# The end of attention in another order, two low parts moved from POOL to DVE, and a sum of two products kept in PSUM

## The chip, the cores and the metric

The kernel runs on one core of one Trainium2 chip. The time is the device time of one execution in microseconds (us), over everything from the first to the last instruction; the figure for a kernel is the median of several runs. The core's engines are named as in the profile: PE (matmuls), DVE (the vector engine), ACT (the scalar engine, with its function tables), POOL (GpSimd) and SP, which issues the loads. Each engine works through its own list in the order written; engines wait for one another through semaphores. SBUF is the memory on the chip, PSUM the banks that PE writes into.

## The reference

One layer of a decoder trunk on 512 tokens of width 1024, in float32. Three sub-layers, each with a norm before it and a norm after it, and a residual sum:

```python
x = x + 0.5 * rms_norm(swiglu(rms_norm(x, ffn1_pre_g), ffn1_w_gu, ffn1_w_down), ffn1_post_g)
y = hybrid_mixer(rms_norm(x, mix_pre_g), w_in, ..., w_o)
x = x + rms_norm(y, mix_post_g)
x = x + 0.5 * rms_norm(swiglu(rms_norm(x, ffn2_pre_g), ffn2_w_gu, ffn2_w_down), ffn2_post_g)
```

`swiglu` is `(silu(x @ w_gate) * (x @ w_up)) @ w_down` with an inner width of 2816. The mixer projects to five parts with `w_in`: `x_lru` and `gate_lru` (512 columns each), queries (8 heads of 64), keys and values (2 heads of 64). The LRU half is a short convolution, two block-diagonal gates, a linear scan over the tokens, times `gelu(gate_lru)`. The attention half is a causal window of 128 tokens with sinks. Each half has its own norm, and both together are multiplied by `w_o`.

## The kernel before

**Products.** The activations lie transposed, `xT[c]` being 128 features by 512 tokens for c = 0 to 7. Float32 accuracy comes from splitting every operand in a high part (rounded to the matmul's format, by an ACT copy) and a low part (what is left, by a subtraction), and from three matmuls (`mm3`, L358 to L363): high by high, high by low, low by high. Weights pass through class `Weights`: a unit is loaded by SP, rounded by ACT (`round`, L171) and split by the `low` engine (`take_low`, L176). `W.fill(n)` makes the low parts of all units up to n beyond those taken, and calls the loads that follow; where it is called decides where in the list of DVE or POOL the low part stands. Which of the two does it is written beside each unit: for `w_in`'s columns 2 and 3 (`xl`) DVE and POOL, and for the first pair of ffn2's gate and up weights DVE for gate 0 and POOL for up 0, gate 1 and up 1.

**Feed-forward products by quads.** Most of the pairs of hidden chunks go through `quad` (L682), a product by seven 2x2 block products with sums of blocks of weights and of tokens. It uses three banks, A, D and B. `seven` takes a weight unit and runs 24 matmuls into one bank. Block product b11 goes into A and is copied by ACT to `p1` (L691); later b21 goes into B, and a DVE addition (L697) forms `p1 + B`, on which ACT runs the Silu one unit later. There are nine quads in ffn1 (names ending in a) and eight in ffn2 (b).

**Boundaries.** `boundary` (L560) joins a sub-layer's last products to the next sub-layer's first ones. Of the eight output chunks, the last three (5, 6, 7, called late) are made in two halves of 256 tokens. While the three products of half 1 run, half 0 gets its norm: `stats` (four small matmuls on the sum of squares `accb_r`, L406, then a square root on ACT and a reciprocal and a diagonal `dg_r` on DVE), `spread` (L421, a matmul that gives the inverse norm to all partitions), `scale` (L554, DVE), `add` (L558, the residual sum, DVE for even chunks and POOL for odd ones) and `high` (L431, ACT, the high part of the next input, `xh_mx` or `xh_f`). Calls are put between the row steps of a product by `hooks`: a product has `n` steps of three matmuls, n = 6 at the first boundary (ffn1 to mixer) and 8 at the second (mixer to ffn2). Then `k_high` (L374) runs the next sub-layer's first four products row by row: for each row k it multiplies the high part of that row by high and low parts of the four weight units, eight matmuls a row; the low parts of the rows follow in `k_low`. In row steps 0 to 3, `k_high` starts as soon as `xh` of row 0 is there, and takes rows 1 to 3 as they come.

**The end of attention.** Eight units of scores, softmax and values run in a software pipeline (L1292 on), with the last weight products of the gate (`gt`) between them on PE. Beside them the LRU half goes on: the scans (L1172, four of them, `scan(2)`, `scan(3)`, then `scan(0)` and `scan(1)`), and gelu of the gate in four steps which end in `G` (L1128) for chunks 0 and 1. `run_due` issues what has been put off to a given unit; `deferred` holds one subtraction, the low part `wlo_wo` of the fourth chunk of `w_o` (L157), to be issued by `deferred.run()`. After the last unit, `invert_rms` scales the four blocks `yn` by their norm (L1287), PE transposes them (`atp`, L1338), ACT and DVE make high and low parts (`yah`, `yal`), POOL multiplies the scans by G or gt (L1364), and DVE sums the squares in `acc_lru` (L1358), for which PE's statistics `rms_lru` (L406) wait. PE works on the attention rows of `w_o` in between (L1380, L1383).

Of the kernel before, what the change touches and what calls it, by code (L numbers as in the profile page):

```python
# [11 lines left out]
AF = mybir.ActivationFunctionType  # L12
# [7 lines left out]
KD = D // P  # L20
F = 2816
# [90 lines left out]
def tile_layer(ctx: ExitStack, tc: tile.TileContext, out: bass.AP, **ins: bass.AP):  # L112
# [73 lines left out]
        return add_pair([src[0, r0 * P:(r0 + nk) * P, c * P:(c + 2) * P]], nk, f"{name}{c}_", low)  # L186

    def add_gate_up(w_gu, f, name):
        g, u = (add_cols(w_gu[:, :, o:o + F], f, KD, f"{name}{s}", 0, (dve, dve) if f else (dve if s == "g" else pool, pool))
                for s, o in (("g", 0), ("u", F)))  # L190
        for j in range(2):
            g[j]()
            u[j]()
# [47 lines left out]
    O2 = 2 * C  # L241
    O3 = O2 + C
    for c in (0, 2):
        for add in add_cols(w_in, c, KD, "xl", 0, (dve, pool)):
            add()
    for add in add_pair([w_in[0, :, O3:O3 + 2 * P]], KD, "kv"):
        add()
# [123 lines left out]
            mm3(ps[:, sl], w, k, [t[:, sl] for t in x], k == 0, k == len(xs) - 1)  # L371
        return ps

    def k_high(ws, banks, xs, sl, ks):  # L374


        for k in ks:
            xh = xs[k][0][:, sl]
            for (hi, lo), ps in zip(ws, banks):
                pe.matmul(ps[:, sl], hi[:, k, :], xh, start=k == 0, stop=False)  # L380
                pe.matmul(ps[:, sl], lo[:, k, :], xh, start=False, stop=False)  # L381

    def k_low(ws, banks, xs, sl):
        n = len(xs)
# [119 lines left out]
    class Residual:  # L504
# [48 lines left out]
            y = self.ys[c][:, HALF[h]]  # L553
            dve.scalar_tensor_tensor(y, y, self.gain(c), bc, op0=ALU.mult, op1=ALU.mult)  # L554

        def add(self, c, h):
            sl = HALF[h]
            (pool if c % 2 else dve).tensor_add(xT[c][:, sl], self.ys[c][:, sl], xT[c][:, sl])  # L558

    def boundary(res, late, xs, parts, nxt, name):  # L560

        for i, (c, w) in enumerate(late):
            b = product(w, xs, HALF[0], f"{name}y{c}0")
            res.late(c, b, parts and parts[c], 0)
            res.late_square(c, 0)
            res.late_add(0, i == 0)
            W.fill((2, 3, 3)[i])

        def steps(ks, h, bc):
            for k in ks:  # L570
                res.scale(k, h, bc)
            for k in ks:
                res.add(k, h)
            for k in ks:
                nxt.high(k, h)

        bcs = [None, None]

        def spread(h):
            bcs[h] = res.rms[h].spread()  # L580

        def spread_a():
            spread(0)
            steps((0, 1), 0, bcs[0])

        n = len(xs)
        hooks = [{}, {1: res.rms[0].stats, 3: lambda: W.fill(4), n - 2: spread_a}, {}]
        for i, (c, w) in enumerate(late):
            b = product(w, xs, HALF[1], f"{name}y{c}1", hooks[i])
            if i == LATE - 1:  # L590
                for k in (2, 3):
                    res.scale(k, 0, bcs[0])
                res.add(2, 0)
                res.add(3, 0)
                res.late_add(1, False)
            res.late(c, b, parts and parts[c], 1)
            if i == LATE - 1:
                nxt.high(2, 0)
            res.late_square(c, 1)
            if i == 0:  # L600
                res.late_add(1, True)
        res.scale(4, 0, bcs[0])
        res.late_add(1, False)
        nxt.high(3, 0)
        res.scale(5, 0, bcs[0])
        for k in (4, 5):
            res.add(k, 0)
        for k in (4, 5):
            nxt.high(k, 0)
        ws = [W.take(0) for _ in range(4)]  # L610
        banks = [bank(f"{name}n{i}") for i in range(4)]
        k_high(ws, banks, nxt.xs, HALF[0], range(0, 4))
        for k in (6, 7):
            res.scale(k, 0, bcs[0])
        for k in (6, 7):
            res.add(k, 0)
        res.rms[1].stats()
        for k in (6, 7):
            nxt.high(k, 0)
        for k in range(KD):  # L620
            nxt.low(k, 0)
        k_high(ws, banks, nxt.xs, HALF[0], range(4, 6))
        spread(1)
        for k in range(0, KD, 2):
            steps((k, k + 1), 1, bcs[1])
        nxt.sum_squares(0)
        k_high(ws, banks, nxt.xs, HALF[0], range(6, 8))
        k_low(ws, banks, nxt.xs, HALF[0])
        for k in range(KD):
            nxt.low(k, 1)  # L630
        W.fill(2)
        nxt.sum_squares(1)
        k_high(ws, banks, nxt.xs, HALF[1], range(8))
        k_low(ws, banks, nxt.xs, HALF[1])
        return banks


    class Hidden:
# [24 lines left out]
        def quad(self, f, last, ahead):  # L663
# [24 lines left out]
            A, D, B = (bank(f"{s}{n}") for s in "adb")  # L688
            p1, p7, u2, u4, g1 = (wt(f"{s}{n}") for s in ("p1", "p7", "u2", "u4", "g1"))
            seven(A, "b11", True)  # L690
            act.copy(p1, A)  # L691
            seven(D, "t3", True)
            act.copy(p7, D)
            seven(A, "t2", False)
            act.copy(u2, A)
            seven(B, "b21", True)
            dve.tensor_add(p1, p1, B)  # L697
            W.later(1, act.activation, p1, p1, AF.Silu)
            seven(A, "t1", False)
            act.copy(u4, A)  # L700
            W.later(1, dve.tensor_add, u4, p7, u4)
# [592 lines left out]
    for now in range(n_units + 2):  # L1294
# [19 lines left out]
        if now == 6:  # L1314
            for ci in range(KC):
                root_u(ci)
            for ci in (2, 3):
                scan(ci)
        if now == n_units:
            scan(0)  # L1320
            deferred.run()
            preload(AF.Sqrt)
            root_rms(slice(0, NB - 1))

# [2 lines left out]
    preload(AF.Exp)  # L1327
    invert_rms(slice(0, NB - 1))
    invert_rms(slice(NB - 1, NB))
    scan(1)  # L1330
    run_due(n_units + 1)
    pump(100)
    ysp = [None] * KD
    gts[KC - 1] = scaled(wt(f"gt{KC - 1}"), gts[KC - 1])
    tps = [bank(f"atp{ci}") for ci in range(KC)]
    for ci, tp in enumerate(tps):
        for b in range(NB):
# [203 lines left out]
```

## Time and profile before

| what | value |
|---|---|
| median of 3 runs | 884.88 us (884.69 to 884.94) |
| the profiled execution's own time | 886.26 us |
| its span, first to last instruction | 884.6 us |
| mean granted clock of PE | 0.997 |
| PE busy | 873.8 us, 99% |
| DVE busy | 668.5 us, 76%, 993 instructions |
| ACT busy | 459.5 us, 52%, 791 instructions |
| POOL busy | 129.0 us, 15%, 117 instructions |
| DMA, mean over the span | 98 GB/s |

The profiled execution took 1.38 us more than the median of the unprofiled runs. Times in the timeline count from the start of its span. A line of a timeline has the start, the duration, the engine, the source line, the operation, output and inputs, and in square brackets the idle time ahead of it with what ended it. Matmuls overlap: the time between the starts of two, not their duration, is what one costs (0.12 us for 256 columns, 0.23 us for 512). A line of the waits has the engine and operation that waited, what it waited for, the sum, the number and the longest. A line of the groups has the busy time, the mean of one in ns, and the idle time of the engine ahead.

### The profile page before, as it was taken

The numbers are of one execution on the slowest core, as the hardware profiler recorded it, in microseconds if no ns is written. First come the engines' busy times: TensorE is split into PE (matmuls) and PEld (weight loads), VectorE is DVE, ScalarE is ACT, GpSimd is POOL, SyncE is SP. The second block draws the span as 40 slices with busy tenths as digits, with TensorE's granted clock in tenths as the row PEclk, the third lists the DMA queues.
The fourth block names the chain that finished last, engine by engine and source line by source line (L and its number), as shares of the span: only waits on it lengthen the run. The fifth ranks groups of instructions, "written<-read, shape, count | busy, mean of one in ns | idle before, by whom it ended". The sixth has DMA issues, their size and how long they took to land.

```text
span 884.6 us, 14243 instructions
## 1 busy us (share of the span) xinstructions
PE 873.8 (99%) x5768; PEld 801.5 (91%) x5768; DVE 668.5 (76%) x993; ACT 459.5 (52%) x791; POOL 129.0 (15%) x117
## 2 busy tenths in 40 slices
PE   8999999999999999999999999999999999999997
PEld 8988999989989998998887899888998998998996
DVE  4979758778778864889999679588677677777754
ACT  6646534544535554457787346535463452552542
POOL 2010000000000015435463154210000000000013
PEclk9999999999999999999999999999999999999999
DMA  7242243152242253332301130224232241261212
GB/s 240 73 152 83 92 142 103 54 162 72 73 142 97 84 167 96 96 96 76 115 1 49 60 131 5 93 95 143 96 127 65 96 145 46 96 190 37 86 46 96
DMA packets 83553, 86.68 MB, mean 98 GB/s; under 512 B 3664, under 2 KB 75680, under 8 KB 83488
## 3 DMA queue, kind: packets, MB, share of 16 engines
q1 hardware_dynamic: 83312, 85.64, 30.2%
q8 instruction: 45, 0.74, 0.3%
q14 instruction: 20, 0.16, 0.1%
q10 hardware_dynamic: 144, 0.13, 0.0%
q0 software_dynamic: 32, 0.00, 0.0%
HBM read 83.67 MB, written 2.10 MB: 97 GB/s over the span
## 4 chain that ended last, share of the span: by engine, by line
PE 91%; DVE 5%; ACT 2%; issue 1%; DMA 1%; POOL 0%; SPq 0%; POOLq 0%; DVEq 0%; ACTq 0%
PE aa L676 12%; PE ab L676 10%; PE da L676 6%; PE db L676 5%; PE ya L361 4%; PE ya L362 4%; PE ya L363 4%; PE yb L1426 4%; PE yb L1427 4%; PE yb L1425 4%; PE ba L676 3%; PE bb L676 3%; PE a_first L841 1%; PE an L380 1%; PE mn L380 1%; PE mn L387 1%
## 5 line engine op out<-in xcount | busy, mean ns | idle before, releaser
L361 PE MATMUL ya<-hha,whi_ad 128*128 128x512 f32 x158 | 61.5, 389 | 0.0
L362 PE MATMUL ya<-hla,whi_ad 128*128 128x512 f32 x158 | 61.5, 389 | 0.0
L363 PE MATMUL ya<-hha,wlo_ad 128*128 128x512 f32 x158 | 61.5, 389 | 0.0
L1425 PE MATMUL yb<-whi_bd,hhb 128*128 128x512 f32 x144 | 56.1, 389 | 0.0
L1426 PE MATMUL yb<-wlo_bd,hhb 128*128 128x512 f32 x144 | 56.1, 389 | 0.0
L1427 PE MATMUL yb<-whi_bd,hlb 128*128 128x512 f32 x144 | 56.0, 389 | 0.0
L1495 POOL TENSOR_TENSOR yp_b<-yp_b,grow 128x512 f32<-128x512 f32 (+1 forms) x8 | 9.7, 1222 | 282.0 <-ACT ysq L1489 282.0
L942 POOL MEMSET bd_w_rg<- 128x512 f32 x1 | 0.5, 528 | 266.0 <-PE aa L676 266.0
L363 PEld LDWEIGHTS ya<-hha,wlo_ad 128*128 128x128 f32 x158 | 29.7, 188 | 6.2
L361 PEld LDWEIGHTS ya<-hha,whi_ad 128*128 128x128 f32 x158 | 29.7, 188 | 6.1
L362 PEld LDWEIGHTS ya<-hla,whi_ad 128*128 128x128 f32 x158 | 29.7, 188 | 6.0
L1427 PEld LDWEIGHTS yb<-whi_bd,hlb 128*128 128x128 f32 x144 | 27.0, 188 | 5.6
L1425 PEld LDWEIGHTS yb<-whi_bd,hhb 128*128 128x128 f32 x144 | 27.0, 188 | 5.6
L1426 PEld LDWEIGHTS yb<-wlo_bd,hhb 128*128 128x128 f32 x144 | 27.0, 188 | 5.5
L176 DVE TENSOR_TENSOR wlo_bd<-raw_bd,whi_bd 128x1024 fp32r<-128x1024 f32 x22 | 26.4, 1219 | 3.6 <-ACT whi_bd L171 3.6
L171 ACT CAST whi_bd<-raw_bd 128x1024 fp32r<-128x1024 f32 x22 | 22.9, 1049 | 5.1 <-PE bb L676 3.8
L1446 DVE TENSOR_TENSOR yp_b<-yb,yp_b 128x512 f32<-128x512 f32 x24 | 16.4, 692 | 11.6 <-PE yb L1427 11.6
L1000 DVE TENSOR_TENSOR yp_a<-ya,yp_a 128x512 f32<-128x512 f32 x24 | 16.4, 686 | 8.8 <-PE ya L363 8.8
L697 DVE TENSOR_TENSOR p1a<-p1a,ba 128x512 f32<-128x512 f32 x9 | 6.2, 688 | 21.7 <-PE ba L676 21.7
L697 DVE TENSOR_TENSOR p1b<-p1b,bb 128x512 f32<-128x512 f32 x8 | 5.5, 688 | 18.2 <-PE bb L676 18.2
L380 PE MATMUL an<-xh_mx,whi_xl 128*128 128x256 f32 x64 | 15.9, 289 | 0.0
L381 PE MATMUL an<-xh_mx,wlo_xl 128*128 128x256 f32 x64 | 15.5, 283 | 0.0
(1523 smaller groups left out, 3418.4 us busy)
## 6 DMA issues: line engine op xcount, KB each, us to landing
raw_bd<-in_ffn_w_down SPq DMA_DIRECT2D x10, 1024.0 KB, 6.8
xn<-in_x SPq DMA_DIRECT2D x8, 256.0 KB, 4.6
raw_q<-in_w_in SPq DMA_DIRECT2D x4, 512.0 KB, 3.8
out_dram<-yp_b SPq DMA_DIRECT2D x7, 256.0 KB, 2.0
first<-in_ffn_w_gu SPq DMA_DIRECT2D x4, 256.0 KB, 5.1
raw_second<-in_ffn_w_gu SPq DMA_DIRECT2D x2, 512.0 KB
raw_ag__104<-in_ffn_w_gu SPq DMA_DIRECT2D x1, 1024.0 KB
raw_au__286<-in_ffn_w_gu SPq DMA_DIRECT2D x1, 1024.0 KB, 5.8
```

Source lines behind the costliest of these rows:

```text
L171: act.copy(two(hi, x), x)
L176: low.tensor_sub(two(lo, x), x, two(hi.bitcast(F32), x))
L361: pe.matmul(ps, hi[:, k, :], xh, start=start, stop=False)
L362: pe.matmul(ps, hi[:, k, :], xl, start=False, stop=False)
L363: pe.matmul(ps, lo[:, k, :], xh, start=False, stop=stop)
L380: pe.matmul(ps[:, sl], hi[:, k, :], xh, start=k == 0, stop=False)
L676: pe.matmul(o, w[:, k, js], x, start=first and i + j + k == 0, stop=k == 3 and i == 2, skip_group_check=True)
L1000: dve.tensor_add(parts[c], b, parts[c])
L1425: pe.matmul(ps, hh[:, blk], hi[:, k, cs], start=start, stop=False)
L1426: pe.matmul(ps, hh[:, blk], lo[:, k, cs], start=False, stop=False)
L1427: pe.matmul(ps, hl_[:, blk], hi[:, k, cs], start=False, stop=stop)
L1446: dve.tensor_add(parts[tb, dh], ybanks[tb], parts[tb, dh])
```

## The change

1. In a quad, ACT copies A (b11) into bank B, not into `p1`, and b21 accumulates on it; the DVE addition goes, and Silu reads bank B.
2. The low part of the second unit of `w_in`'s columns 2 and 3 is made by DVE, and so are those of gate 1 and up 1 of ffn2's first pair. Up 0 stays with POOL.
3. At the boundaries, half 0's statistics are issued a row step later. The first `fill` in half 1's second product becomes `fill(3)` and a rounding; `fill(4)` moves into `spread_a`, behind the two first rows. There scale, add and high go row by row, and both adds are DVE's. At the first boundary `spread_a` moves from step 4 of half 1's second product to step 1 of its third; at the second it stays at step 6 of the second.
4. At the second boundary, `fill` between the products of half 0 reaches two units and not up to three, and the next unit is rounded after them.
5. `k_high` takes rows 0 to 3 with seven matmuls each, leaving out the low part of the fourth unit, and runs its four matmuls behind them.
6. At the end of attention, what is due (G of chunk 1) is issued ahead of `scan(0)`, `deferred.run()` behind the scaling of `yn`, and `scan(1)` behind the scaling of the last gate chunk.

```diff
@@ -186,7 +186,7 @@
         return add_pair([src[0, r0 * P:(r0 + nk) * P, c * P:(c + 2) * P]], nk, f"{name}{c}_", low)
 
     def add_gate_up(w_gu, f, name):
-        g, u = (add_cols(w_gu[:, :, o:o + F], f, KD, f"{name}{s}", 0, (dve, dve) if f else (dve if s == "g" else pool, pool))
+        g, u = (add_cols(w_gu[:, :, o:o + F], f, KD, f"{name}{s}", 0, (dve, dve) if f or s == "g" else (pool, dve))
                 for s, o in (("g", 0), ("u", F)))
         for j in range(2):
             g[j]()
@@ -241,7 +241,7 @@
     O2 = 2 * C
     O3 = O2 + C
     for c in (0, 2):
-        for add in add_cols(w_in, c, KD, "xl", 0, (dve, pool)):
+        for add in add_cols(w_in, c, KD, "xl", 0, (dve, dve if c else pool)):
             add()
     for add in add_pair([w_in[0, :, O3:O3 + 2 * P]], KD, "kv"):
         add()
@@ -371,14 +371,18 @@
             mm3(ps[:, sl], w, k, [t[:, sl] for t in x], k == 0, k == len(xs) - 1)
         return ps
 
-    def k_high(ws, banks, xs, sl, ks):
+    def k_high(ws, banks, xs, sl, ks, late=None):
 
 
         for k in ks:
             xh = xs[k][0][:, sl]
-            for (hi, lo), ps in zip(ws, banks):
+            for i, ((hi, lo), ps) in enumerate(zip(ws, banks)):
                 pe.matmul(ps[:, sl], hi[:, k, :], xh, start=k == 0, stop=False)
-                pe.matmul(ps[:, sl], lo[:, k, :], xh, start=False, stop=False)
+                if i != late:
+                    pe.matmul(ps[:, sl], lo[:, k, :], xh, start=False, stop=False)
+        if late is not None:
+            for k in ks:
+                pe.matmul(banks[late][:, sl], ws[late][1][:, k, :], xs[k][0][:, sl], start=False, stop=False)
 
     def k_low(ws, banks, xs, sl):
         n = len(xs)
@@ -553,18 +557,22 @@
             y = self.ys[c][:, HALF[h]]
             dve.scalar_tensor_tensor(y, y, self.gain(c), bc, op0=ALU.mult, op1=ALU.mult)
 
-        def add(self, c, h):
+        def add(self, c, h, eng=None):
             sl = HALF[h]
-            (pool if c % 2 else dve).tensor_add(xT[c][:, sl], self.ys[c][:, sl], xT[c][:, sl])
+            (eng or (pool if c % 2 else dve)).tensor_add(xT[c][:, sl], self.ys[c][:, sl], xT[c][:, sl])
 
     def boundary(res, late, xs, parts, nxt, name):
 
+
+        n = len(xs)
         for i, (c, w) in enumerate(late):
             b = product(w, xs, HALF[0], f"{name}y{c}0")
             res.late(c, b, parts and parts[c], 0)
             res.late_square(c, 0)
             res.late_add(0, i == 0)
-            W.fill((2, 3, 3)[i])
+            W.fill(2 if n > 6 else (2, 3, 3)[i])
+        if n > 6:
+            W.round()
 
         def steps(ks, h, bc):
             for k in ks:
@@ -581,10 +589,21 @@
 
         def spread_a():
             spread(0)
-            steps((0, 1), 0, bcs[0])
-
-        n = len(xs)
-        hooks = [{}, {1: res.rms[0].stats, 3: lambda: W.fill(4), n - 2: spread_a}, {}]
+            for k in (0, 1):
+                res.scale(k, 0, bcs[0])
+                res.add(k, 0, dve)
+                nxt.high(k, 0)
+            W.fill(4)
+
+        def fill_a():
+            W.fill(3)
+            W.round()
+
+        hooks = [{}, {2: res.rms[0].stats, 3: fill_a}, {}]
+        if n > 6:
+            hooks[1][n - 2] = spread_a
+        else:
+            hooks[2][1] = spread_a
         for i, (c, w) in enumerate(late):
             b = product(w, xs, HALF[1], f"{name}y{c}1", hooks[i])
             if i == LATE - 1:
@@ -609,7 +628,7 @@
             nxt.high(k, 0)
         ws = [W.take(0) for _ in range(4)]
         banks = [bank(f"{name}n{i}") for i in range(4)]
-        k_high(ws, banks, nxt.xs, HALF[0], range(0, 4))
+        k_high(ws, banks, nxt.xs, HALF[0], range(0, 4), 3)
         for k in (6, 7):
             res.scale(k, 0, bcs[0])
         for k in (6, 7):
@@ -688,14 +707,13 @@
             A, D, B = (bank(f"{s}{n}") for s in "adb")
             p1, p7, u2, u4, g1 = (wt(f"{s}{n}") for s in ("p1", "p7", "u2", "u4", "g1"))
             seven(A, "b11", True)
-            act.copy(p1, A)
+            act.copy(B, A)
             seven(D, "t3", True)
             act.copy(p7, D)
             seven(A, "t2", False)
             act.copy(u2, A)
-            seven(B, "b21", True)
-            dve.tensor_add(p1, p1, B)
-            W.later(1, act.activation, p1, p1, AF.Silu)
+            seven(B, "b21", False)
+            W.later(1, act.activation, p1, B, AF.Silu)
             seven(A, "t1", False)
             act.copy(u4, A)
             W.later(1, dve.tensor_add, u4, p7, u4)
@@ -1317,8 +1335,8 @@
             for ci in (2, 3):
                 scan(ci)
         if now == n_units:
+            run_due(n_units)
             scan(0)
-            deferred.run()
             preload(AF.Sqrt)
             root_rms(slice(0, NB - 1))
 
@@ -1327,11 +1345,12 @@
     preload(AF.Exp)
     invert_rms(slice(0, NB - 1))
     invert_rms(slice(NB - 1, NB))
-    scan(1)
+    deferred.run()
     run_due(n_units + 1)
     pump(100)
     ysp = [None] * KD
     gts[KC - 1] = scaled(wt(f"gt{KC - 1}"), gts[KC - 1])
+    scan(1)
     tps = [bank(f"atp{ci}") for ci in range(KC)]
     for ci, tp in enumerate(tps):
         for b in range(NB):
```

The low products named in 3 are, in the profile's names, `wlo_xl` at the first boundary and `wlo_bg` and `wlo_bu` at the second.

## The prediction

> **What bounds the kernel now.** I read the shares of the engines and the chain that ended last, then PE's own waits, then, engine by engine, the timeline around the places that the change touches.
>
> ```profile
> PE 873.8 (99%) x5768; PEld 801.5 (91%) x5768; DVE 668.5 (76%) x993; ACT 459.5 (52%) x791; POOL 129.0 (15%) x117
> PE 91%; DVE 5%; ACT 2%; issue 1%; DMA 1%; POOL 0%; SPq 0%; POOLq 0%; DVEq 0%; ACTq 0%
> ...
> L697 DVE TENSOR_TENSOR p1a<-p1a,ba 128x512 f32<-128x512 f32 x9 | 6.2, 688 | 21.7 <-PE ba L676 21.7
> L697 DVE TENSOR_TENSOR p1b<-p1b,bb 128x512 f32<-128x512 f32 x8 | 5.5, 688 | 18.2 <-PE bb L676 18.2
> ...
> PE rms_lru L406 <- DVE acc_lru L1358: 0.7, 1, 0.7
> PE rms_r L406 <- DVE accb_r L550: 0.5, 1, 0.5
> PE atp L1338 <- DVE yn L1287: 0.3, 1, 0.3
> PE rms_r L421 <- ACT whi_xl L171: 0.2, 1, 0.2
> ```
>
> PE is the bound: busy 99%, on 91% of the chain. No PE wait on a quad or on POOL's low parts is listed, and the four waits above are all that the change can take away; their listed sum is 1.7 us. So the change can win little, and it loses wherever it makes PE wait for something new. That is decided where rows have little slack, at the first boundary (starts in us, then durations):
>
> ```profile
> 358.40 0.67 PE L421 MATMUL rms_r<-dg_r,ones 128*128 128x256 f32 x2 [0.21 <-ACT whi_xl L171]
> 361.78 0.28 PE L380 MATMUL an<-xh_mx,whi_xl 128*128 128x256 f32 x1
> ...
> 358.37 2.39 POOL L176 TENSOR_TENSOR wlo_xl<-raw_xl__3697,whi_xl 128x1024 fp32r<-128x1024 f32 x1 [4.84 <-ACT whi_xl L171]
> 359.11 0.88 DVE L554 SCALAR_TENSOR_TENSOR yp_a<-yp_a,half_g,rms_r 128x256 f32<-128x256 f32 x2 [0.85 <-PE rms_r L421]
> 359.90 1.14 DVE L558 TENSOR_TENSOR xT<-yp_a,xT 128x256 f32<-128x256 f32 x1
> 361.30 0.86 DVE L554 SCALAR_TENSOR_TENSOR yp_a<-yp_a,half_g,rms_r 128x256 f32<-128x256 f32 x2
> 362.08 0.41 DVE L558 TENSOR_TENSOR xT<-yp_a,xT 128x256 f32<-128x256 f32 x1
> 362.53 0.51 ACT L431 ACTIVATE xh_mx<-xT,cols 128x256 fp32r<-128x256 f32 x1
> 364.13 0.49 ACT L431 ACTIVATE xh_mx<-xT,cols 128x256 fp32r<-128x256 f32 x1
> ...
> 515.95 1.73 DVE L550 TENSOR_TENSOR accb_r<-accb_r,sq_r 128x256 f32<-128x256 f32 x1 [0.48 <-ACT sq_r L392]
> 517.73 0.61 PE L406 MATMUL rms_r<-mean_d,accb_r 128*128 128x1 f32 x4 [0.50 <-DVE accb_r L550]
> ...
> 467.80 1.20 DVE L157 TENSOR_TENSOR wlo_wo<-raw_wo__4578,whi_wo 128x1024 fp32r<-128x1024 f32 x1
> 468.91 1.79 DVE L1128 SCALAR_TENSOR_TENSOR G<-sq_g,gt 128x512 f32<-128x512 f32 x1
> ```
>
> See that the matmuls of the next stage start at 361.78 with the first row's high part just made, that rows 2 and 3 are high at 363.04 and 364.62 for a PE that wants them at 363.70 and 364.66, and that DVE operations on SBUF are long when a POOL operation runs beside them: the add at 359.90 took 1.14 us until just after POOL's 2.39 ended, against 0.41 at 362.08.
>
> **The quads.** 17 additions (9 x 688 ns and 8 x 688 ns, 11.7 us of DVE) go. DVE sat idle ahead of them (21.7 and 18.2 us, all for PE), and 24 matmuls of a quad's product take 2.88 us with no wait between products. Worth nothing to PE: 0. ACT's copy has the same count and now lands in bank B, where the next product to write is three products of 2.88 us later; the copy is hidden by these. If that cover failed, each quad would pay about one copy (a rival below). SP's queue and the order of loads are as before.
>
> **First boundary (ffn1 to mixer).** Gains first. PE lost 0.23 us ahead of the statistics (356.06 to 356.41, where rows are 0.12 apart), and 0.36 + 0.08 at the spread (357.92 to 358.40, then 0.32 to the next row where the second boundary shows 0.24). Both go, since the statistics come 3 x 0.12 later and the spread a product later: -0.67, so the next stage could start at 361.78 - 0.67 = 361.11.
>
> Now the price, followed along DVE, which runs its list in order. Product 7 started at 359.62; without the stalls and without the spread in front of it (it adds 0.42: gaps 0.12, 0.24, 0.30 for two of 0.12) it starts at 358.53. The spread follows its first three rows, at 358.89, and the first scale 0.63 later (520.06 to 520.69 at the second boundary), at 359.52; before, 359.11. Then scale 0.47, add 0.41, scale 0.47, add 0.41 with the joints of the trace (0.03 to 0.04 where one needs the other, -0.08 where not): the second add ends at 361.27. Rows 0 and 1 are in time (high parts by 361.0 and 361.8, needed 361.11 and 361.95). But the fill behind them puts the low part wlo_xl, which POOL did in 2.39 us, on DVE: 1.22 us (mean of 22 such of wlo_bd, 1219 ns), 361.19 to 362.41. Queued behind it are the scales of rows 2 and 3 and add 2, which so starts at 363.12 (before 362.08). ACT follows 0.45 after it and is done at 364.08; PE, at seven matmuls a row (0.84), wanted row 2 at 362.79: a stall of 1.31. Row 3's high part began 2.05 after add 2 in the trace (POOL's add 0.86, the square's sum, the next copy and the square ahead of it on ACT), so is ready at 365.66 for a PE that wants it at 364.94: 0.74. Row 3 and the four low matmuls put behind take 0.84 + 0.48, to 367.00, against 365.74 before: **+1.3**. Ends: +0.8, if POOL's add no longer stretches the square's sum (0.85 to 0.43); +1.9, if the spread still waits 0.45 for its diagonal. What follows on DVE moves by 1.0 and is in time. Moving four low matmuls behind helps only by 4 x 0.12 of work before the next gap; it does not reach 1.31.
>
> The Trainium skill (SBUF — State Buffer, section "SBUF: two separate sides") says of DVE with two SBUF inputs and POOL that whichever starts first holds their shared ports for its whole instruction and the other fully blocks. The row at 359.90 agrees with that, and it speaks for taking the low part from POOL. By that rule alone the change would win the 0.73 that this add lost; the sum above has that already, since its add takes 0.41.
>
> **Second boundary (mixer to ffn2).** The accumulation at 515.95 lasted until POOL's low part was through (1.73 for 0.42), and the statistics began at 517.73 where PE was there at 517.07: 0.66, gone after, with two low parts now on DVE. The spread stays in its place, 0.66 sooner. One low part lies ahead of scale 0 (its cover: DVE idles 1.18 there), one again behind add 1: add 2 begins about 524.0 against 523.36. PE now starts the stage at 523.42, row 2 is in time, and row 3, by the same 2.04 from add 2 and 0.5 on ACT, is ready at 526.6 to 526.7 for 525.94: about 0.7. Net **+0.1**, ends -0.7 and +0.8.
>
> **End of attention.** The transposes wait 0.20 + 0.28 + 0.48 = 0.96 for yn (gaps of 0.31, 0.39, 0.59 for 0.11); with G (1.79, but 0.68 at 454.94, beside no POOL work) ahead of the scan and wlo_wo (1.2) and the second scan behind, yn is early and these go. But the same DVE list must still end in acc_lru, and PE then waits for that (483.08 to 484.20, 0.89 over the 0.23 spacing). Without meetings, the list ends thus: the last values let yn start at 469.1 instead of 470.92, and 13.22 us of work from there, less the 0.67 that POOL put on one row, plus 1.15 for wlo_wo give 482.8, where before without its 1.77 of meetings it would be 482.4. POOL's four products with G and gt (1.29 each alone) now start later and meet the scales of yn, the low part and the gelu rows. Two to four meetings of about 0.65 give 484.1 to 485.4, against 484.14: I take **+0.4**, near the lower third, as two is what before had. Ends: -0.9 (the whole wait at the statistics goes) and +1.3.
>
> **Sum.** 0 + 1.3 + 0.1 + 0.4 = +1.8 us. On the profiled execution's own 886.26 us (span 884.6) that is 888.06; this execution was 1.38 above the median of the runs, so I carry the difference: 884.88 + 1.8 = **886.7 us**.
>
> **Rivals.**
> - Faster: rows 2 and 3 are in time at the first boundary. It needs add 2 to begin by 361.8 rather than 363.1, so DVE would have to hide the 1.22 us of wlo_xl; DVE's idle 0.4 ahead of the spread speaks for it, the order of the list against. Then the boundary gives -0.67, the second -0.66 and attention -0.5 to -0.9: about -2.0, 882.9.
> - Same: attention gives what the first boundary takes. If the meetings stay away, -0.9 + 1.3 + 0.1 = +0.5, 885.4. For it: the 1.1 that G loses now. Against: the same POOL work only moves.
> - Slower still: meetings at the upper end and the spread late, 1.9 + 0.5 + 1.3 = +3.7, 888.6.
> - Bank B is not free when ACT copies, or the copy is late for b21: 17 x 0.57 (ACT's copy of a bank at 457.08) = +9.7, 894.6. Three products of cover speak against it.
> - The clock: a stall might make PE slow. The granted clock is 0.997 with waits up to 1.4 us, so waits of 1.31 and 0.74 should not; a half-rate stretch of 3.4 us would add 1.7 to my sum: 888.4.
>
> The Trainium skill (TensorE: Matmul & The Clock Gate, section "Part 1: The HAM clock gate") puts the fall to half rate after an idle window of about 3.4 us, more than any stall here. No row of this trace shows such a fall.
>
> **How the numbers follow.** About 0.2% (1.77 us) is what a measurement of this kernel tells from no change; my forecast lies on that border. The forecast (+1.2 to +2.8, 886.1 to 887.7) gets 0.53, of it 0.35 over the border; the same-rival 0.19; faster 0.13; slower still 0.10; bank 0.03; clock 0.02. Slower: 0.35 + 0.15 = 0.50; same: 0.18 + 0.19 = 0.37; faster 0.13. The range leaves out most of faster, the bank, and the tail of slower still: 884.0 to 888.5.
>
> **What would show it.** Right: PE waits for xh_mx (ACT L431) of 1.3 and 0.7 near 363 to 366, for xh_f of 0.7 near 527; none ahead of the boundary statistics, the spread or atp; a longer wait at rms_lru; accb_r and G near their short times; no wait in the quads. Wrong: rows 2 and 3 in time, or PE waiting for an ACT copy in a quad.

## The result and the profile after

The changed kernel takes 888.53 us (median of 6 executions, 886.84 to 890.17), against 884.68 us before in the same comparison: a ratio of 1.0042, 95% interval 1.0031 to 1.0053. By the two medians it is 3.85 us slower, by the ratio 3.7. The forecast was 886.7 us with a range from 884.0 to 888.5: the direction is right, the time stands on the upper edge of the range (0.03 us past the figure given), and the loss is twice the +1.8 us of the sum. The six times lie 3.3 us apart, where those of before lie within 0.5 us; the lower the granted clock of PE (0.999 to 0.995), the longer the time. The profiled execution is the shortest, 886.84 us with a span of 885.1 us, so what it shows is the change at full clock: the granted clock is 1.00 from the first matmuls to the last.

The shares of the engines and of the chain that ended last, then PE's waits, in the profile of the changed kernel:

```profile
PE 873.3 (99%) x5768; PEld 800.5 (90%) x5768; DVE 663.0 (75%) x981; ACT 458.8 (52%) x791; POOL 117.9 (13%) x112
...
PE 93%; DVE 5%; ACT 1%; issue 1%; POOL 0%; POOLq 0%; DVEq 0%; ACTq 0%
```

```profile
PE an L380 <- ACT xh_mx L435: 1.6, 2, 1.2
...
PE rms_lru L410 <- DVE acc_lru L1377: 1.4, 1, 1.4
PE wo L1402 <- DVE yal L438: 0.6, 2, 0.4
PE mn L380 <- ACT xh_f L435: 0.5, 1, 0.5
```

The four waits of before, for the statistics, the spread and atp, are gone or have turned: two new ones for the rows of the first boundary, one for those of the second, a new one for yal, and one at the LRU statistics that has doubled. POOL does 11 us less, DVE 5.5 us less; neither is worth anything to PE.

Where the time went is best read by counting PE's matmuls in order of their starts (from 0; 5768 in either kernel) and setting the starts of the same one side by side. Where the text says "by position", it means a change in this distance to before:

| matmul, in which stage | before, us | after, us | after less before | change since the row above |
|---|---|---|---|---|
| 20, start | 6.01 | 6.00 | -0.01 | |
| 150, first products | 24.54 | 22.81 | -1.73 | -1.72 |
| 2380, ahead of the first boundary | 353.42 | 351.69 | -1.73 | 0.00 |
| 2550, behind it | 374.99 | 374.55 | -0.44 | **+1.29** |
| 3140, ahead of attention's end | 469.59 | 469.11 | -0.48 | -0.04 |
| 3250, behind it | 493.86 | 494.37 | +0.50 | **+0.98** |
| 3600, behind the second boundary | 542.21 | 542.77 | +0.56 | **+0.06** |
| 5760, last | 877.18 | 877.74 | +0.56 | 0.00 |

Nothing moved in the quads (matmuls 150 to 2380, 3600 to 5760). The 1.73 us at the start have nothing to do with the change. In windows of time (start and end, length, PE's busy time and count, granted clock, DMA share and GB/s) the profiled execution of before has, from 8 to 12 us,

```profile
8.00:12.00 4.00, 4.00 (x18) 0.57 1.12 339
```

and that of the changed kernel

```profile
8.00:12.00 4.00, 4.00 (x34) 1.00 1.15 346
```

so the former ran there at about half clock. That is the 1.4 us by which it stood above its median, and the way it was carried in the sum was right. Against that, the waits of the change cost 1.29 + 0.98 + 0.06 = 2.3 us, which is what its shortest executions show (886.84 for 884.5). The other 1.4 to 1.5 us of the median goes with the lower clock, and the experiments had to find whose that is.

The first boundary in the changed kernel, DVE, ACT and PE (start, duration):

```profile
359.05 0.42 DVE L562 TENSOR_TENSOR xT<-yp_a,xT 128x256 f32<-128x256 f32 x1
359.39 1.22 DVE L176 TENSOR_TENSOR wlo_xl<-raw_xl__3688,whi_xl 128x1024 fp32r<-128x1024 f32 x1
360.53 0.87 DVE L558 SCALAR_TENSOR_TENSOR yp_a<-yp_a,half_g,rms_r 128x256 f32<-128x256 f32 x2
361.31 0.42 DVE L562 TENSOR_TENSOR xT<-yp_a,xT 128x256 f32<-128x256 f32 x1
...
361.76 0.51 ACT L435 ACTIVATE xh_mx<-xT,cols 128x256 fp32r<-128x256 f32 x1 [1.74 <-DVE xT L562]
...
363.35 0.49 ACT L435 ACTIVATE xh_mx<-xT,cols 128x256 fp32r<-128x256 f32 x1
...
362.32 0.39 PE L380 MATMUL an<-xh_mx,whi_xl 128*128 128x256 f32 x1 [1.16 <-ACT xh_mx L435]
...
363.89 0.39 PE L380 MATMUL an<-xh_mx,whi_xl 128*128 128x256 f32 x1 [0.47 <-ACT xh_mx L435]
```

This is the list of the prediction, shifted by the 1.73 us: the low part of 1.22 us between the second add and the scales of rows 2 and 3, and PE losing 1.32 and 0.63 us over its spacing, that is, the gap between two starts less the usual one (1.31 and 0.74 were forecast).

The end of attention and the second boundary in the changed kernel:

```profile
466.18 0.68 DVE L1146 SCALAR_TENSOR_TENSOR G<-sq_g,gt 128x512 f32<-128x512 f32 x1
...
468.56 0.69 DVE L1289 TENSOR_TENSOR yn<-po,rden 128x512 f32<-128x512 f32 x1 [0.47 <-PE po L1282]
...
469.55 2.15 DVE L1305 TENSOR_SCALAR yn<-yn,rat 128x512 f32<-128x512 f32 x3
...
472.21 1.22 DVE L157 TENSOR_TENSOR wlo_wo<-raw_wo__4569,whi_wo 128x1024 fp32r<-128x1024 f32 x1
...
476.86 1.66 DVE L1139 TENSOR_TENSOR sq_g<-sq_g,gt 128x512 f32<-128x512 f32 x1
...
483.95 0.69 DVE L1377 TENSOR_TENSOR acc_lru<-acc_lru,sq_l 128x512 f32<-128x512 f32 x1 [0.46 <-DVE acc_lru L1377]
...
516.51 0.43 DVE L554 TENSOR_TENSOR accb_r<-accb_r,sq_r 128x256 f32<-128x256 f32 x1 [0.55 <-ACT sq_r L396]
...
522.21 1.22 DVE L176 TENSOR_TENSOR wlo_bu<-raw_bu__5437,whi_bu 128x1024 fp32r<-128x1024 f32 x1
```

In the profile of before, the scales of yn and the same gelu row were

```profile
471.73 1.28 DVE L1287 TENSOR_SCALAR yn<-yn,rat 128x512 f32<-128x512 f32 x3
...
477.67 0.69 DVE L1121 TENSOR_TENSOR sq_g<-sq_g,gt 128x512 f32<-128x512 f32 x1
```

G takes 0.68 instead of 1.79 us and accb_r 0.43 instead of 1.73, as expected of operations that POOL no longer holds up. But the list still ends 0.98 later on PE's own time: three scales of yn take 2.15 (1.28 before) and one gelu row 1.66 (0.69), each beside one of POOL's products (469.33 and 476.50), and ahead of the last addition to acc_lru DVE sat idle 0.46 us with no releaser but itself.

### The profile page after: what moved, and what is told of

It reads as the page before. It is cut to its first block, busy times and chain, and to the rows that moved or that the text cites. A ratio compares the mean times of both kernels' runs of the same rounds, so it can differ in the third digit from the quotient of the medians.

```text
span 885.1 us, 14253 instructions
## 1 busy us (share of the span) xinstructions
PE 873.3 (99%) x5768; PEld 800.5 (90%) x5768; DVE 663.0 (75%) x981; ACT 458.8 (52%) x791; POOL 117.9 (13%) x112
## 4 chain that ended last, share of the span: by engine, by line
PE 93%; DVE 5%; ACT 1%; issue 1%; POOL 0%; POOLq 0%; DVEq 0%; ACTq 0%
PE aa L695 12%; PE ab L695 10%; PE da L695 6%; PE db L695 5%; PE ya L361 4%; PE ya L362 4%; PE ya L363 4%; PE yb L1444 4%; PE yb L1446 4%; PE yb L1445 4%; PE ba L695 3%; PE bb L695 3%; PE a_first L859 1%; PE mn L391 1%; PE an L391 1%; PE pgb L361 1%
## 5 line engine op out<-in xcount | busy, mean ns | idle before, releaser
L531 POOL TENSOR_TENSOR acca_r<-acca_r,sq_r 128x512 f32<-128x512 f32 x6 | 8.4, 1405 | 48.0 <-ACT sq_r L396 48.0
L361 PE MATMUL gt<-xh_mx,whi_gt 128*128 128x512 f32 x32 | 14.2, 444 | 0.0
```

The source lines that it names most:

```text
L361: pe.matmul(ps, hi[:, k, :], xh, start=start, stop=False)
```

## The experiments

### One part at a time

Theory one: the four parts add up as waits (0, +1.3, +0.1, and now +1.0 for attention), and the rest is a clock that has nothing to do with the change. Theory two: PE's new waits themselves cost clock. The changed kernel was run again, and each part alone on top of the kernel before, all on one chip.

> The changed kernel once more, unaltered, for the spread of its times. Its six executions so far lie between 886.84 and 890.17 us and their mean granted clock between 0.999 and 0.995, the slower the lower; those of before lie between 884.43 and 884.94. Theory one (the sum by waits): the waits alone are +2.3 us, and what is above 887 us is a lower clock that has nothing to do with the change, so here most executions should be near 887. Theory two (the clock): the new waits of PE near 361 and 363 us make the clock fall in some executions; then the times again spread over 3 us and more, and a profile of an execution above 888 shows the clock fall right behind the first boundary.

Measured: 886.96, 887.27, 888.36, 889.02 and 889.14 us, at clocks of 0.999, 0.998, 0.997, 0.997 and 0.997; ratio 1.0035 [1.0023, 1.0048]. Two of five are near 887; the spread is there again, and on a chip where 22 of 27 executions of before were between 884.4 and 885.2. The profiled one was the shortest again, so it shows no fall.

The quads alone:

```diff
-            act.copy(p1, A)
+            act.copy(B, A)
-            seven(B, "b21", True)
-            dve.tensor_add(p1, p1, B)
-            W.later(1, act.activation, p1, p1, AF.Silu)
+            seven(B, "b21", False)
+            W.later(1, act.activation, p1, B, AF.Silu)
```

> Before, with the change in the quads alone (ACT copies b11 into bank B, no addition on DVE). Theory one: 0, so 884.4 to 884.9 us, DVE busy 11.7 us less, no PE wait in the quads. Rival (PE waits for the copy or the bank): up to 17 x 0.57 = +9.7 us. If the spread of the whole change's times came from the quads, it shows here.

Measured: 884.80 us against 884.89, ratio 1.0000 [0.9991, 1.0009]; one of 11 above 885.2. From matmul 150 to the last, PE's distance to before stays at -1.28 to -1.34 us. The quads are worth nothing and cost nothing.

The order at the end of attention alone:

```diff
+            run_due(n_units)
             scan(0)
-            deferred.run()
...
-    scan(1)
+    deferred.run()
     run_due(n_units + 1)
     pump(100)
     ysp = [None] * KD
     gts[KC - 1] = scaled(wt(f"gt{KC - 1}"), gts[KC - 1])
+    scan(1)
```

> Before, with the new order at the end of attention alone. By the trace of the whole change this part takes +0.96 us (PE 0.48 ahead of the old kernel's distance at matmul 3140 and 0.50 behind at 3250); theory one: +0.9 to +1.0, so 885.6 us, PE waits for acc_lru 1.4 to 1.6 us instead of 0.9 and for yal, none for atp. Rival: part of it is due to the 1.3 us by which the first boundary shifts PE and DVE; then it is below +0.5 here. Theory two on the clock: times tight, clock as in before.

Measured: 886.04 us, ratio 1.0019 [1.0010, 1.0029]. By PE's positions the part costs +0.47 us (-1.72 ahead of it, -1.25 behind), not +0.96; PE's waits:

```profile
PE rms_lru L406 <- DVE acc_lru L1359: 1.1, 1, 1.1
...
PE po L1264 <- POOL pa L1251: 0.3, 1, 0.3
...
PE wo L1384 <- DVE yal L434: 0.2, 1, 0.2
```

The times fall into groups: six between 885.2 and 886.1, three between 887.1 and 887.5 (clock 0.997), two at 888.7 and 889.3 (0.994). Groups some 1.5 and 3.3 us above the first speak for theory two, at the LRU statistics, though a loss at the start (1.4 us in the profile of before) would look like the first of them.

The boundaries alone, with all that the diff has there, `k_high` and the two engines of the low parts included:

```diff
-            steps((0, 1), 0, bcs[0])
+            for k in (0, 1):
+                res.scale(k, 0, bcs[0])
+                res.add(k, 0, dve)
+                nxt.high(k, 0)
+            W.fill(4)
...
-        k_high(ws, banks, nxt.xs, HALF[0], range(0, 4))
+        k_high(ws, banks, nxt.xs, HALF[0], range(0, 4), 3)
```

> Before, with everything at the boundaries (statistics a step later, fills, spread at the first boundary a product later, low parts on DVE, four low matmuls behind) and nothing else. Theory one: +1.3 at the first and +0.1 at the second, 886.1 us, with PE waits of 1.3 and 0.6 for xh_mx and 0.65 for xh_f. Theory two (the clock): besides, some executions are 1.5 to 3 us longer at a clock of 0.996 or less, and the times spread as those of the whole change do.

Measured: 886.43 us, ratio 1.0017 [1.0009, 1.0026]; +1.31 us at the first boundary and +0.05 at the second by PE's positions. Four of 11 have a clock of 0.997 or less, but so have 13 of the 77 executions of before whose clock is known; and the one that was profiled had its loss at the start. Whether waits of 1.3 and 0.6 us at this place cost clock is not decided by this.

### Is it the wait that costs the clock?

Two kernels took the waits by themselves: before, with useless DVE work ahead of the LRU statistics or ahead of rows 2 and 3, and nothing of the change.

```diff
     for ci in range(KC):
         add_square(ci)
+    for _ in range(3):
+        dve.tensor_scalar(accl, accl, 1.0, None, op0=ALU.mult)
```

> Before, with nothing of the change, but three multiplications of acc_lru by 1.0 on DVE ahead of the LRU statistics, so that PE waits about 1.3 us longer there (0.9 to 2.2 us); the output stays the same. It asks whether a longer wait of PE at this place by itself lowers the granted clock, as the spread of attn_only (885.2 to 889.3 us, clock 0.998 to 0.994) suggests. Theory one (waits only): +1.3 us, 886.1 us, and the spread of before (884.4 to 885.2, and one in five at 886.2). Theory two (a wait in PE can cost clock): on top of +1.3 most executions lose 1.5 us or a multiple of it, so a median of 887.5 us or more at a clock of 0.997 or lower, and a profile of such an execution has a granted clock under 1 right behind 483 us.

Measured: 885.74 and 885.93 us at clock 0.999; 887.40, 887.71, 887.79 at 0.996 to 0.997; 889.22 at 0.994; ratio 1.0027 [1.0015, 1.0038]. The profile is of one of 887.71 us. Its PE, then its windows (the fourth number is the granted clock):

```profile
484.06 1.05 PE L406 MATMUL rms_lru<-mean_c,acc_lru 128*128 128x1 f32 x8 [2.12 <-DVE acc_lru L1370]
...
485.52 0.40 PE L1382 MATMUL wo<-yah,whi_wo 128*128 128x512 f32 x1
...
486.03 0.63 PE L1382 MATMUL wo<-yah,whi_wo 128*128 128x512 f32 x1
486.45 0.63 PE L1382 MATMUL wo<-yah,wlo_wo 128*128 128x512 f32 x1
```

```profile
482.00:484.00 2.00, 0.00 (x0) 1.00 0.02 4
484.00:486.00 2.00, 1.94 (x12) 0.98 0.00 0
486.00:488.00 2.00, 2.00 (x6) 0.50 0.00 0
488.00:490.00 2.00, 2.00 (x7) 0.66 0.05 12
490.00:492.00 2.00, 2.00 (x10) 1.00 0.89 306
```

PE idles 2.27 us over its spacing, 1.38 more than before, runs the statistics and four matmuls of 512 columns, and then goes at half clock for 3.4 us (by the clock's column, 485.9 to 489.4): matmuls of 512 columns 0.43 us apart instead of 0.23, which costs 1.56. By position the kernel loses 2.94 = 1.38 + 1.56 there. Theory two holds at this place: a wait is paid, and in most executions its clock after it.

```diff
             if i == LATE - 1:
+                for _ in range(8 if n == 6 else 0):
+                    dve.tensor_scalar(res.ys[2], res.ys[2], 1.0, None, op0=ALU.mult)
                 for k in (2, 3):
```

Here the tile is finished before and multiplied by one, so the output is that of the kernel before.

> Before, with nothing of the change, but eight multiplications of one finished tile by 1.0 on DVE (about 0.41 us each) ahead of the scales of rows 2 and 3 at the first boundary, so that PE waits for row 2's high part there; the output is not used otherwise. Waits alone: 8 x 0.41 less the 0.66 us by which row 2 was early, about +2.6 us, 887.4 us. If a wait of PE at this place costs clock as the one at the LRU statistics did (lru_wait: 512-column rows 0.43 us apart instead of 0.23 from 486.0 to 489.0 us), most executions are 1.5 us or more above that, 889 us, and the profile has 256-column rows about 0.2 us or more apart behind the wait. If it does not, the clock's loss in the whole change comes from the LRU statistics alone.

Measured: 890.93 us (889.47 to 892.24), ratio 1.0066 [1.0053, 1.0079], none of five with a clock above 0.996. The wait is 3.3 us and not 2.6. The windows of the profiled execution:

```profile
364.00:366.00 2.00, 0.00 (x0) 1.00 0.79 239
366.00:368.00 2.00, 0.94 (x4) 0.61 0.00 0
368.00:370.00 2.00, 2.00 (x11) 0.50 0.00 0
370.00:372.00 2.00, 2.00 (x11) 0.50 0.00 0
372.00:374.00 2.00, 2.00 (x14) 0.68 0.00 0
```

Of the +6.0 us at this place, 3.3 are the wait and some 2.7 the clock. So a wait at the first boundary costs clock too if it is long enough: all of five executions lost clock with 3.3 us here, four of six with 2.3 us at the LRU statistics.

### Which waits of the change can be had back

The low part of the first boundary, made where DVE is idle between the diagonal and the spread:

```diff
         else:
+            hooks[1][5] = lambda: W.fill(4)
             hooks[2][1] = spread_a
```

> The boundary parts alone, as in boundary_only, but at the first boundary the low part wlo_xl is made a product sooner, between the diagonal and the spread, where DVE is idle, and not between the rows. Theory one: scale 0 begins 0.4 later, but rows 2 and 3 stand behind 1.22 us less: the waits for xh_mx shrink from 1.32 + 0.63 to about 0.3 to 0.5 + 0.7, and the boundary costs +0.5 and not +1.3: 885.6 us at full clock. Rival (rows 2 and 3 are late for the moved spread, not for the low part): the waits stay as they are and the time is that of boundary_only.

Measured: 885.29 us, ratio 1.0004 [0.9995, 1.0013], and all 11 within 884.9 to 886.1 at 0.998 or 0.999. At the first boundary +0.56 instead of +1.31. PE's waits:

```profile
PE an L380 <- ACT xh_mx L435: 0.7, 2, 0.5
PE mn L380 <- ACT xh_f L435: 0.5, 1, 0.5
```

Over PE's spacing they are 0.34 at row 0, 0.18 at row 2 and 0.64 at row 3. So it is the low part that made row 2 late (1.32 before this call), and 0.75 us of the 1.3 hang on the one call's place. Row 3 waits as long as in the whole change (0.63), so its delay does not hang on the low part: its high part again begins 2.05 us after the add of row 2 (360.95 and 363.00), the distance that the prediction used.

G's place alone, the first line of the diff of attention:

```diff
+            run_due(n_units)
             scan(0)
             deferred.run()
```

> Before, with only G of chunk 1 issued ahead of the scan at the end of attention; wlo_wo and the second scan keep their places. Theory one: G loses its 1.1 us beside POOL, wlo_wo (1.2 us) lies where DVE would otherwise sit idle for the last values (1.12 us in attn_only), so the whole list ends 0.6 to 1.2 us sooner: no wait for atp, a wait for acc_lru of 0.9 or less, 883.9 us. Rival: POOL's products only meet other rows, and the list ends where it did: within 0.3 us of before. If the part costs as attn_only does (+0.5), it is G's place and not that of wlo_wo that costs.

Measured: 884.87 us, ratio 0.9999 [0.9990, 1.0008]; -0.21 us by position. Even that is hardly G: in this profile PE waited 0.48 us at po for POOL's pa, as in fill_ahead and row_wait, where nothing of attention is changed and the same stretch came out 0.16 shorter than before. So G's place is worth some 0.05. The rival, that POOL's products only meet other rows, fits the rows of this profile: G still takes 1.06 us, and the three scales of yn now take 2.32 (1.28 before). By difference, what costs in attn_only is the rest, wlo_wo and the scan moved behind.

The whole change with the low part ahead, the diff of fill_ahead on top of the change:

> The whole change, with the low part of the first boundary made a product sooner as in fill_ahead. By waits: quads 0, first boundary +0.55, second +0.05, attention +0.5 (as in attn_only) or +1.0 (as in the whole change): 885.9 to 886.4 us at full clock, against 887.0 for the best executions of the whole change. By the clock: the waits of the first boundary no longer cost any, so fewer executions are slow, but those that lose it at the LRU statistics (wait 1.2 to 1.5 us) stay: a median of 886.5 to 888 us. If attention takes +0.5 here, it was the boundary's shift that made it +1.0 in the whole; if +1.0, something else did.

Measured: 887.02 us, ratio 1.0028 [1.0017, 1.0039]; four executions at 886.0 to 886.4, three at 887.7 to 888.3, one at 890.21, which is the profiled one. Its PE lost 1.59 us over its spacing at the LRU statistics, and then its clock:

```profile
PE rms_lru L410 <- DVE acc_lru L1378: 1.4, 1, 1.4
```

```profile
484.00:486.00 2.00, 1.08 (x8) 0.87 0.01 4
486.00:488.00 2.00, 2.00 (x6) 0.50 0.00 0
488.00:490.00 2.00, 2.00 (x6) 0.50 0.00 0
490.00:492.00 2.00, 2.00 (x6) 0.50 0.45 114
492.00:494.00 2.00, 2.00 (x10) 0.93 1.06 364
```

This is the change's own wait, and the half clock lasts 6.8 us (485.5 to 492.3). By position PE stands at -0.25 ahead of this place and at +3.88 behind it: 4.1 us, of which 0.98 are the waits as in the changed kernel and some 3.2 the clock. There was no fall behind the first boundary.

Why one execution loses clock and another does not can be narrowed down in the kept traces. Within each of them the changes of the granted clock lie whole multiples of 3.413 us apart: 105 of them between the falls at 8.05 and 366.45 in row_wait, 116 between 485.94 and 881.88 in lru_wait, 117 between 485.46 and 884.82 in whole_fill_ahead (the last two falls come when PE has no more work). In the profile of the changed kernel the clock falls only at 883.68, after the last matmul, and 117 steps ahead of it lies 484.32. The table takes the stretch between two such points around each wait:

| run, wait | stretch, us | PE busy in it, us | clock in the next |
|---|---|---|---|
| row_wait, row 2 | 363.03 to 366.45 | 0.90 | 0.50 |
| lru_wait, LRU statistics | 482.53 to 485.94 | 1.88 | 0.50 |
| whole_fill_ahead, LRU statistics | 482.05 to 485.46 | 1.98 | 0.50 |
| boundary_only, rows 2 and 3 | 363.32 to 366.74 | 1.90 | 1.00 |
| changed kernel, LRU statistics | 480.91 to 484.32 | 2.37 | 1.00 |

In whole_fill_ahead the wait lies inside one stretch; in the changed kernel's profile the same wait (482.92 to 484.70) is cut by the point at 484.32, and the clock held. So where a wait lies between these points is a candidate for what decides, but few profiles bear on it, and the busy time does not sort the cases alone: with 1.90 us, the rows of boundary_only lost nothing. The only wait of the change that a kept trace shows with a fall behind it is the one at the LRU statistics; whether its waits at the first boundary cost clock in other executions stays open.

### The second half of attention's cost

Attention cost 0.98 in the whole change and 0.47 alone. The difference is the idle 0.46 us ahead of the last addition to acc_lru, in all three profiles of the whole change and its variant with the low part ahead, and in none of the runs with a part of it. Two runs asked whether it hangs on the place in DVE's list or on the first boundary's shift.

```diff
+                for _ in range(8):
+                    dve.memset(scr, 0.0)
             A, D, B = (bank(f"{s}{n}") for s in "adb")
```

> The whole change plus eight tiny DVE memsets of one column in a quad of ffn1, where DVE is idle, so that all later DVE instructions stand eight places further on in its list. In the three profiles of the whole change DVE sat idle 0.46 us ahead of the last addition to acc_lru, with nothing that it waited for, and in no kernel with part of the change. If that idle hangs on the place in DVE's list, it now falls on an instruction some eight places earlier, and the last addition follows the second as elsewhere (2.28 us for the three); if it hangs on what runs beside it (ACT, POOL, the table load), it stays where it is.

Measured: 886.64, 888.17, 889.66 and 890.09 us, ratio 1.0049 [1.0033, 1.0066]. The idle is gone:

```profile
482.21 2.28 DVE L1381 TENSOR_TENSOR acc_lru<-acc_lru,sq_l 128x512 f32<-128x512 f32 x3
```

and attention takes +0.43 us. But it is not found eight places earlier either, and this execution also had PE's wait at po (0.46), which those with the idle lacked.

Boundaries and attention without the quads:

> Boundaries and attention's end without the quads. If the quads matter for attention's cost only by shifting DVE's list, the idle of 0.46 us ahead of the last addition to acc_lru is absent here, and attention takes +0.5 as in attn_only, not +1.0: best executions at 884.6 + 1.35 + 0.5 = 886.5 us. If the first boundary's shift of PE and DVE is what makes it +1.0, the idle is there and the best executions are at 887.0.

Measured: 888.11 us, ratio 1.0037 [1.0023, 1.0051], the shortest 886.63 and 886.64. The three additions take 2.28 us, attention +0.48, the first boundary +1.30. So the first boundary's shift is not what doubled attention's cost, and the two best executions stand where the sum of the parts puts them. What makes the idle, the place in the list or the meeting of DVE and POOL near 463 us, stays open: both changed together.

### What is left as a gain

> What the runs so far leave as gains, put together: the quads, G ahead of the scan with all else of attention's end as before, the first boundary as before, and at the second boundary the statistics a step later with gate 1's low part on DVE, while up 1's stays on POOL and the rows are taken as before. By waits: 0 - 0.2 (g_early) - 0.4 (the wait of 0.66 for the statistics goes, the diagonal and the add beside POOL give some of it back) = -0.6 us, 884.2 us. Rival: the second boundary ends where it did, as rows 2 and 3 are late instead: -0.2, not to be told from before.

Measured: 884.29 us against 884.85, ratio 0.9995 [0.9987, 1.0004]. By position -0.65 us, nearly all at the second boundary, where PE no longer waits for accb_r; of its waits in the middle of the kernel there remain

```profile
PE rms_lru L406 <- DVE acc_lru L1364: 0.7, 1, 0.7
...
PE atp L1344 <- DVE yn L1292: 0.3, 1, 0.3
PE rms_r L421 <- ACT whi_xl L171: 0.2, 1, 0.2
```

It is the shortest kernel by its median and eight of its 11 executions are below 884.4, but the interval holds no change.

## Why the prediction was right, and where it was not

**The quads, 0:** right. 1.0000, no wait in a quad, 11.7 us of DVE gone for nothing. One reading in it was off, without effect: b21 starts two products after b11 ends (da at 83.03, aa at 85.91, ba at 88.79 in the profile of before), so the copy's cover is 5.76 us and not three products.

**First boundary, +1.3:** right, +1.29 in the change and +1.31 alone, by the mechanism named. The two stalls of 1.31 and 0.74 measured 1.32 and 0.63. The rival in which rows 2 and 3 are in time needed DVE to hide 1.22 us; it did not. fill_ahead shows that it could have, but also that this would not have made the rival true: row 3 still waited 0.64, and the boundary cost +0.56 where the rival had -0.67.

**Second boundary, +0.1:** right, +0.06: the 0.66 at the statistics went, and row 3 waits 0.65 (0.7 forecast).

**End of attention, +0.4:** the mechanism was right (longer wait at the LRU statistics, none for atp) and the size was off, +0.98 being within its ends. The sum took yn at 469.1 us on before's time, and it came at 468.56 + 0.48 = 469.04. It took 13.22 - 0.67 + 1.15 = 13.70 us of work from there, and acc_lru was ready at 484.64 + 0.48 = 485.12, so 2.38 us were meetings and idle. The mis-sized term is "two to four meetings of about 0.65": with 482.8 and 484.14 + 0.4, the sum left 1.74 us for them. There were two, the scales of yn (0.87) and a gelu row (0.97), 1.84 us together, then the idle of 0.46, which no row of before foretold, and 0.1 of waiting for the square root. As a part alone, at +0.47, the term was right.

**Sum at full clock, +1.8:** the waits are +2.3, and the difference of 0.5 is for the most part that idle.

**The clock, 0.02:** here the prediction failed. It argued that waits of 1.31 and 0.74 us should not lower the clock, since waits of up to 1.4 us were in the profile of before, and looked only at the first boundary. But the 1.4 us wait is in the first microseconds, before there is work, and says nothing of a wait in mid-kernel. The trace did show a fall, against the sentence "No row of this trace shows such a fall": the clock is 0.50 from 8.25 to 11.67 us, behind two waits of PE of 0.5 and 0.7 us, and that is where the mean of 0.997 and the 1.4 us over the median come from. And the longest new wait was at the LRU statistics, 1.55 us over the spacing, which the prediction had listed as longer and not priced again. Seven of the 11 executions of the changed kernel had a clock of 0.997 or less. The price named for the rival (888.4 us) is, within 0.2 us, the median that came, though as +2.3 us of waits and 1.4 to 1.5 of clock and not as +1.8 and 1.7. That the median still stands on the edge of the range is luck: the range's upper end was set for more meetings and a late spread, not for the clock. With that case at 0.5 rather than 0.02, the same sum would have given 886.7 at full clock and 888.4 with one fall.

The rule that the prediction set beside it, from the Trainium skill (TensorE: Matmul & The Clock Gate, section "Part 1: The HAM clock gate"), was a fall after an idle window of about 3.4 us, "more than any stall here". These runs do not agree with it in that form: PE idled 1.6 us over its spacing in whole_fill_ahead, 2.3 in lru_wait, and the clock fell to 0.50 in both, 0.5 and 1.9 us after work had begun again. What the page says besides, that the window runs freely, fits the grid of the clock's changes above and that only some executions of the same kernel lose; stretches of 3.4 and 6.8 us at half clock are one window and two of the page's 3.4. The measurement decides here: 1.6 us is enough, at times.

The other rule, of the Trainium skill (SBUF — State Buffer, section "SBUF: two separate sides"), spoke for the change. It agreed with the rows once more (G 1.79 to 0.68, accb_r 1.73 to 0.43 with POOL away), and with the change slower all the same: the lost time of a blocked operation is only worth something if its list was the one that PE waited for.

## What to carry to other kernels

Where PE is busy 99% of the time, a piece of work put on an in-order engine between two rows that PE takes one by one delays the rows behind it by its full length (1.22 us here); the same piece one step earlier, where that engine idles, cost PE 0.75 us less. Price every new wait of PE twice, as the wait and as a chance of 1.5 us or more of half clock behind it, and see in the spread and the granted clock of several executions, not in the one profiled, whether it happened. Counting matmuls and setting the starts of the same one side by side tells in one table which stage of a long kernel took what, apart from the luck of the start.

## What the runs showed of the hardware that was not expected

- A single wait of PE in mid-kernel can be followed by 3.4 or 6.8 us at half clock (0.50). In lru_wait (2.3 us) the fall began 1.9 us after the wait's end and cost 1.56 us; in whole_fill_ahead (1.6 us) it began 0.5 us after and cost some 3.2; in row_wait (3.3 us) it began within the wait and cost some 2.7. It happens in some executions of a kernel and not in others: in four of six at 2.3 us, in all of five at 3.3 us. Waits of 0.9 us at the LRU statistics, as in before, did not spread the times.
- In the kept traces the changes of the granted clock lie whole multiples of 3.413 us apart, and the half-clock stretches in mid-kernel are one or two of these long (3.41 and 6.83 us).
- The start of the kernel has such a stretch in some executions (0.57 from 8 to 12 us in the profile of before), worth 1.3 to 1.7 us. Of 77 further executions of before, 13 had a clock of 0.997 or less; that theirs was lost at the start too is not shown.
- At the end of attention the same program comes out in two ways, with PE waiting 0.48 us at po for POOL or not; the stretch as a whole differs by some 0.16 us.
- DVE sat idle for 0.46 us ahead of an addition whose inputs were ready, in every profile of the whole change and its variant, and no longer after eight memsets had been put in front. Its cause is open.
